# Padding the attention's matmuls of a streaming encoder layer to full 128x128 array tiles

## The chip, the cores and the metric

The kernel runs on one core of a Trainium2 chip. The metric is the device time of one execution in microseconds (us); the time before the change is the median of three runs. TensorE (PE in the profile) multiplies a stationary block, which a weight load (LDWEIGHTS, PEld in the profile) brings into its array of 128 rows and 128 columns, with a moving block that streams past. The contraction runs over the array's rows, the output partitions over its columns. VectorE is DVE, ScalarE is ACT, GpSimd is POOL, and SyncE (SP) issues most transfers.

## The reference

One inference step of one layer (model width 1024). The input is projected once; eight *latent* heads (low-rank keys and values, a rotary key of 32 shared by all heads, mask by chunks of 64) and eight *forgetting* heads (causal, plus a running sum of log forget gates as a bias) attend, both outputs go through one output projection, and a gated feed-forward network follows.

```python
def attend(q, k, v, scale, valid, bias=None):
    s = jnp.einsum('bqhd,bkhd->bhqk', q, k).astype(jnp.float32) * scale
    if bias is not None:
        s = s + bias
    if valid is not None:
        s = jnp.where(valid, s, NEG_INF)
    p = jax.nn.softmax(s, axis=-1).astype(v.dtype)
    return jnp.einsum('bhqk,bkhd->bqhd', p, v)
...
o_a = attend(q_mla, k_mla, v_mla, MLA_SCALE, chunk_mask)
o_b = attend(f_q, f_k, f_v, FOX_SCALE, causal_mask, fox_bias(cum_q, cum_k))
x = x + concat(o_a, o_b) @ w_out
h = rms_norm(x, norm_ffn)
x = x + (silu(h @ w_gate) * (h @ w_up)) @ w_down
```

There are 1072 token columns: 32 new sample rows (with 512 cached keys of their own), 16 meta rows and 1024 prompt rows. The step returns the outputs and the new rows of the caches.

## The kernel before

Every factor is kept as a high and a low part in a reduced 32-bit format, and a product is the sum of three: high by high, high by low, low by high. Heads have a width of 64, so the parts can share the contraction: `fetch` (line 379) loads for each head `a1`, the high query parts twice (128 rows), and `b1`, the high key parts above the low ones (128 rows). One matmul then gives two of the three products. The third, low query by high key, uses `a2`. For a forgetting head `a2` has 70 rows (64 of the low queries and 6 of bias and mask), against `x`. For a latent head `a2` is used with 64 rows, against the upper half of `b1`, and a third matmul of 106 rows adds the rotary part and the masks:

```python
ops = [(a1, b1, 128), (a2, b1, 64), (x, None, 106)]
...
ops = [(a1, b1, 128), (a2, x, 70)]
```

`scores` (line 538) computes the scores of one query tile and one head: the queries are the stationary block, the keys stream past in segments of up to 456 columns. There are nine query tiles (`QT`): the first holds the 48 sample and meta rows, the others 128 prompt rows each. Tile 0 meets 560 keys, tile i meets 16 + 128 i. So a head has 2 segments for tile 0 and 1, 1, 1, 2, 2, 2, 2 and 3 for the others. In forgetting heads line 566 adds a triangle to the last block of 128 (48 in tile 0). DVE then takes the maximum of each row, ACT the exponential with its sum.

`values` (line 593) multiplies the probabilities with the values for a group of query tiles: (5, 6, 7, 8), then (1, 2, 3, 4), then (0,). Each block of 128 keys is transposed on PE (line 624), split in its two parts by ACT and DVE, and multiplied with the values (lines 640 and 641) two blocks later, through a queue. The 16 meta keys come last: a transpose of 32 columns, the low parts laid below the high ones at row 32, and one product of 48 contraction rows (line 638) against the block `v[:, 13]`, which POOL zeroes (line 410) and two transfers fill. Tile 0 has a path of its own: five transposes of 48 rows (line 600) and products of 112 rows (line 610).

`finish_pair` (line 657) divides by the row sums: their inverses are spread and transposed on PE (line 679), 48 rows for tile 0.

`attention` (line 698) runs the heads one after the other: scores of one set of query tiles beside the values of the set before, and beside a *filler*. The forgetting heads go first, with `latent_heads` (line 430: queries, keys and values of the latent heads, line 473 for the values) as their filler; the latent heads follow, with half of the output projection (`out_half`, line 517) as theirs. The operands of a head are fetched one head ahead, in two buffers each, on SP's queue. The forgetting values come from lines 371 to 373, in the input projection before attention.

The order of the work on each engine isn't that of the code: the framework sets it when the program is built, from its own estimate of when each instruction can start.

Of the kernel before, what the change touches and what calls it, by code (L numbers as in the profile page):

```python
# [9 lines left out]
F32 = mybir.dt.float32  # L10
# [13 lines left out]
T = S_NEW + N_META + SEQ          # token columns: [sample new 32 | meta 16 | prompt 1024]  # L24
ODD = S_NEW + N_META              # first query tile: sample and meta rows
NK = PAST + T                     # key columns: [past 512 | token columns]
# [9 lines left out]
NEG = -2.0 ** 100                # exact in every type it passes through  # L36
# [7 lines left out]
OB = 112                          # key block of the first query tile  # L44
# [4 lines left out]
def trunk(ctx: ExitStack, tc: tile.TileContext, a):  # L49
# [30 lines left out]
    zeros = cst.tile([32, 1], F32, name="zeros")  # L80
# [3 lines left out]
    # scratch, each row as its high and its low part: two heads to a row block  # L84
# [12 lines left out]
    # four slots of 128 rows by 4 * T: the normed input, then the mixed heads, then the normed rows of the FFN  # L97
# [8 lines left out]
    def rsqrt(out, ps, n, dim, pool_):  # L106
        """out = (ps / dim + EPS) ** -0.5: exp(-ln / 2), then one Newton step."""
# [38 lines left out]
    # ------------------------------------------------------------ input projection  # L146
# [6 lines left out]
    with ExitStack() as A:  # L153
# [12 lines left out]
        # every weight goes through one ring of [128, 1024] tiles, in the order of its use  # L166
# [5 lines left out]
        def load_w(upto):  # L172
            while len(ring) < min(upto, len(order)):
                name, m, K, n = order[len(ring)]
                if m is None:
                    # the high parts in rows 0:64 of the product, the low ones in rows 64:128
# [27 lines left out]
        # the normed input without its rstd, which comes in after each product  # L204
# [16 lines left out]
        def low_rank(ws, chunks, dim, gain, out, dst, off):  # L221
            """The rows of some chunks: products, RMS norm over the len(ws) row tiles, split into the scratch."""
# [30 lines left out]
        def background(m):  # L253
            """Caches, split on their way to the scratch."""
# [33 lines left out]
        # decoupled key (rows 0:32) and forget gates (rows 32:40)  # L288
# [16 lines left out]
        with tc.tile_pool(name="krl", bufs=1, side="right") as krl:  # L305
# [5 lines left out]
            # log sigmoid: min(z, 0) - log1p(exp(-|z|)), then its running sum  # L311
# [42 lines left out]
        # low-rank queries  # L354
# [4 lines left out]
        # forgetting values, token rows  # L359
        for half in range(2):  # L360
            w = take(2, 1)
            for i, (t0, n) in enumerate(QT):
# [5 lines left out]
                for k in range(8):  # L368
                    s_hi, s_lo = h_hi(k)[:, t0:t0 + n], h_lo(k)[:, t0:t0 + n]
                    hi, lo = (t[:, k % 4] for t in w[k // 4])  # L370
                    pe.matmul(ps[:n, :256], s_hi, hi, start=(k == 0), stop=False)
                    pe.matmul(ps[:n, :256], s_hi, lo, start=False, stop=False)
                    pe.matmul(ps[:n, :256], s_lo, hi, start=False, stop=(k == 7))
# [5 lines left out]
        def fetch(h):  # L379
# [7 lines left out]
            a2 = hp.tile([70, T], FR, tag="a2", name="a2")  # L387
            move(a2[0:64], sQ[p, rw, 1])
            x = hp.tile([128, NK], FR, tag="x", name="x")
            if h < HEADS:  # L390
# [5 lines left out]
                ops = [(a1, b1, 128), (a2, b1, 64), (x, None, 106)]  # L396
# [9 lines left out]
        def fetch_v(h):  # L406
# [3 lines left out]
            pool.tensor_copy(v[:32, 13], zeros.broadcast_to([32, 128]))  # L410
# [6 lines left out]
    # ------------------------------------------------------------ attention  # L417
# [12 lines left out]
    def latent_heads(ev):  # L430
        """Queries, keys and values of the latent heads, in steps of one product, beside the forgetting heads."""
# [14 lines left out]
        def es(n):  # L446
            """One of three buffers, the first in the free end of the slot."""
            turn[0] += 1
            if turn[0] % 3 == 0:
                return lo[:, 3 * T:3 * T + 2 * n].rearrange("p (j t) -> p j t", j=2)  # L450
            return ev.tile([128, 2, 396], FR, tag="es", name="es")
# [5 lines left out]
        for m in range(6):  # L457
# [10 lines left out]
            else:  # L468
                for kt, (k0, n) in enumerate([(128 * i, 128) for i in range(4)] + [(PAST + t0, n) for t0, n in QT]):
                    ps = psF.tile([128, 512], F32, tag="psF", name="psF")  # L470
                    for k in range(2):
                        s_hi, s_lo = l_hi[:, k, k0:k0 + n], l_lo[:, k, k0:k0 + n]
                        pe.matmul(ps[:n, :256], s_hi, w[0][:, k], start=(k == 0), stop=False)
                        pe.matmul(ps[:n, :256], s_hi, w[1][:, k], start=False, stop=False)
                        pe.matmul(ps[:n, :256], s_lo, w[0][:, k], start=False, stop=(k == 1))
# [41 lines left out]
    def out_half(ev):  # L517
        """x plus the output projection of the forgetting heads, beside the latent heads."""
# [19 lines left out]
    def scores(h, ops, i, rs):  # L538
        t0, nq = QT[i]
# [20 lines left out]
        for si, (out, c, w) in enumerate(segs):  # L560
            tri_here = h >= HEADS and si == len(segs) - 1
            for j, (qa, kb, K) in enumerate(ops):
                kb = mixed["B3"] if kb is None else kb
                last = j == len(ops) - 1
                if last and tri_here:
                    pe.matmul(out[:, w - dg:w], identb[:dg, :dg], trib[:dg, :dg], start=False, stop=False)
# [19 lines left out]
    # products with the values run a few blocks behind the transposes that feed them  # L586
# [6 lines left out]
    def values(h, v, tiles, raw):  # L593
        idx = [i for i, _ in tiles]
        po = None
        if idx == [0]:
            P = tiles[0][1]
            pt = psT.tile([128, 512], F32, tag="psT", name="psT")
            for b in range(5):
                pe.transpose(out=pt[:OB, ODD * b:ODD * b + ODD], in_=P[:ODD, OB * b:OB * b + OB], identity=ident[:ODD, :ODD])  # L600
            t0, n = 0, ODD
            # the high and the low parts side by side, through one product
# [11 lines left out]
        else:  # L614
# [3 lines left out]
            blocks.append((0, 32, v[:32 + N_META, 13], 0))  # L618
            for bi, (c, K, vb, imin) in enumerate(blocks):
# [3 lines left out]
                for g in range(g0, len(tiles)):  # L623
                    pe.transpose(out=pt[:K, 128 * g:128 * g + 128], in_=tiles[g][1][:, c:c + K], identity=ident)  # L624
                if meta:
                    # the low parts below the high ones, through one product; the rows between meet rows of zeros
                    hi, lo = tp.tile([128, 512], FR, tag="pth", name="pth"), None
# [415 lines left out]
```

## Time and profile before

| what | us |
|---|---|
| median of three runs | 1614.98 (1611.57 to 1615.22) |
| span of the profiled execution | 1616.5 |
| PE busy in it | 1560.8 (97%) |
| weight loads (PEld) busy | 1439.6 (89%) |
| DVE busy | 981.4 (61%) |
| ACT busy | 594.1 (37%) |
| POOL busy | 215.0 (13%) |

The profile is of one further execution; its own time is known by its span, 1.5 us (0.1%) above the median of the runs. The stages by time: input projection up to 241 us, the forgetting heads up to about 490 us, the latent heads up to about 752 us, then the output projection and the feed-forward network. Each matmul has two records, the weight load and the matmul; records of neighbours overlap, because the next load and the next matmul start before the last one has ended. So a row's length says little, and the distance between the starts of two rows says what one takes of PE. A timeline row merges neighbours of one line (x2); the shape shown is that of the first.

### The profile page before, as it was taken

Reading aid. Unit: us, or ns where it says so; the run is one execution under the profiler, and the core shown is the slowest. Engines: PE = TensorE matmul, PEld = TensorE weight load, DVE = VectorE, ACT = ScalarE, POOL = GpSimd, SP = SyncE. Lnnn points to the kernel's source line nnn. Section 1 sums busy time; section 2 is a strip of 40 time slices with the busy share of each in tenths; the row PEclk is TensorE's granted clock in tenths of the full one; section 3 lists DMA queues with packets and bytes.
Section 4 is the critical chain, followed back from the end, with each engine's and each line's share of the span. In section 5 each row is a group of like instructions: output and inputs, shape, how many; then the busy total and the mean of one; then the engine's idle time right before and its main releaser. Section 6 shows DMA issues by size and latency. Waiting matters only on the chain.

```text
span 1616.5 us, 24215 instructions
## 1 busy us (share of the span) xinstructions
PE 1560.8 (97%) x9273; PEld 1439.6 (89%) x9273; DVE 981.4 (61%) x1843; ACT 594.1 (37%) x1204; POOL 215.0 (13%) x342
## 2 busy tenths in 40 slices
PE   7999998989999999998999999999999999999995
PEld 6999997867886777776999999999999999999995
DVE  7974616757675656566676556565555656565547
ACT  6443436656664555455451111111111111111124
POOL 1344241422231122020000000000000000000014
PEclk9999999989997999999999999999999999999998
DMA  6588667765875654541611111111111111111003
GB/s 186 185 257 291 189 205 223 249 178 165 236 215 139 157 138 116 136 123 41 208 43 40 40 40 40 40 40 65 53 40 40 40 40 40 66 53 39 27 1 109
DMA packets 87827, 183.07 MB, mean 113 GB/s; under 512 B 9690, under 2 KB 53658, under 8 KB 87620
## 3 DMA queue, kind: packets, MB, share of 16 engines
q1 hardware_dynamic: 70784, 127.24, 27.5%
q0 software_dynamic: 16928, 54.29, 9.6%
q8 instruction: 73, 1.20, 0.3%
q14 instruction: 42, 0.34, 0.1%
HBM read 122.83 MB, written 58.67 MB: 112 GB/s over the span
## 4 chain that ended last, share of the span: by engine, by line
PE 82%; DVE 5%; issue 5%; DMA 4%; ACT 2%; POOL 1%; SPq 0%; DVEq 0%; POOLq 0%; ACTq 0%
PE psG L120 11%; PE psG L119 11%; PE psG L121 11%; PE psS L567 7%; PE psD L857 5%; PE psD L856 5%; PE psD L855 5%; PE psT L624 4%; PE psA L121 3%; PE psA L119 3%; PE psA L120 3%; PE po L640 2%; PE po L641 1%; PE psG L810 1%; PE psG L811 1%
## 5 line engine op out<-in xcount | busy, mean ns | idle before, releaser
L864 DVE TENSOR_TENSOR x<-psD,x 128x408 f32<-128x408 f32 (+1 forms) x496 | 236.4, 523 | 5.7 <-PE psD L857 5.7
L119 PE MATMUL psG<-B_hi,gh 128*128 128x408 f32 (+1 forms) x528 | 172.8, 327 | 0.0
L119 PE MATMUL psG<-A_hi,gh 128*128 128x408 f32 (+1 forms) x528 | 172.6, 327 | 0.0
L120 PE MATMUL psG<-A_lo,gh 128*128 128x408 f32 (+1 forms) x528 | 172.6, 327 | 0.0
L120 PE MATMUL psG<-B_lo,gh 128*128 128x408 f32 (+1 forms) x528 | 172.5, 327 | 0.0
L857 PE MATMUL psD<-ah,dl 128*128 128x408 f32 (+1 forms) x528 | 172.1, 326 | 0.0
L121 PE MATMUL psG<-B_hi,gl 128*128 128x408 f32 (+1 forms) x528 | 171.8, 325 | 0.0
L121 PE MATMUL psG<-A_hi,gl 128*128 128x408 f32 (+1 forms) x528 | 171.8, 325 | 0.0
L856 PE MATMUL psD<-al,dh 128*128 128x408 f32 (+1 forms) x528 | 171.7, 325 | 0.0
L855 PE MATMUL psD<-ah,dh 128*128 128x408 f32 (+1 forms) x528 | 170.9, 325 | 0.1
L844 ACT ACTIVATE sl<-sl 128x408 f32<-128x408 f32 (+1 forms) x66 | 33.1, 502 | 353.7 <-DVE sl L843 353.7
L570 DVE TENSOR_REDUCE nm<-psS 128x1 f32<-128x656 f32 (+2 forms) x144 | 104.5, 726 | 73.5 <-PE psS L567 71.7
L567 PE MATMUL psS<-b,a 128*128 128x328 f32 (+4 forms) x360 | 129.9, 383 | 5.1 <-ACT pb L575 4.1
L66 ACT ACTIVATE pth<-psT 128x512 fp32r<-128x512 f32 (+4 forms) x208 | 98.9, 480 | 87.9 <-PE psT L624 75.4
L67 DVE TENSOR_TENSOR ptl<-psT,pth 128x512 fp32r<-128x512 f32 x192 | 104.5, 553 | 40.5 <-ACT pth L66 38.2
L848 DVE TENSOR_TENSOR sq<-psG,rb 128x408 f32<-128x408 f32 (+1 forms) x66 | 34.9, 529 | 151.9 <-PE psG L121 151.9
L795 POOL TENSOR_TENSOR acc<-acc,sq 128x408 f32<-128x408 f32 x14 | 15.0, 1072 | 811.1 <-ACT sq L794 810.4
L843 DVE TENSOR_TENSOR sl<-psG,rb 128x408 f32<-128x408 f32 (+1 forms) x66 | 35.0, 530 | 122.1 <-PE psG L121 122.1
L567 PEld LDWEIGHTS psS<-b,a 128*128 128x128 f32 x360 | 68.6, 191 | 40.3 <-issue 27.0
L66 ACT ACTIVATE ah<-sl 128x408 fp32r<-128x408 f32 (+1 forms) x66 | 33.2, 503 | 187.4 <-DVE sl L849 129.5
L120 PEld LDWEIGHTS psG<-A_lo,gh 128*128 128x128 f32 x528 | 99.3, 188 | 0.5 <-issue 0.3
L855 PEld LDWEIGHTS psD<-ah,dh 128*128 128x128 f32 x528 | 99.2, 188 | 0.5 <-ACT ah L66 0.3
(271 smaller groups left out, 3877.9 us busy)
## 6 DMA issues: line engine op xcount, KB each, us to landing
sg<-w_gu SPq DMA_DIRECT2D x44, 512.0 KB
a<-sQ SPq DMA_DIRECT2D x48, 268.0 KB
b<-sK SPq DMA_DIRECT2D x32, 396.0 KB
sg<-w_down SPq DMA_DIRECT2D x22, 512.0 KB
v<-sV SPq DMA_DIRECT2D x16, 512.0 KB
wst<-w_in SPq DMA_DIRECT2D x13, 512.0 KB
sV<-vt POOLq DMA_DIRECT2D x24, 256.0 KB, 3.8
sV<-A_hi POOLq DMA_DIRECT2D x24, 256.0 KB, 3.4
```

The lines of the kernel that those rows point to most:

```text
L66: act.activation(hi, src, AF.Copy)
L67: eng.tensor_tensor(out=lo, in0=src, in1=f32(hi), op=ALU.subtract)
L119: pe.matmul(ps, whi(k), rhi(k), start=(k == 0), stop=False)
L120: pe.matmul(ps, whi(k), rlo(k), start=False, stop=False)
L121: pe.matmul(ps, wlo(k), rhi(k), start=False, stop=(k == K - 1))
L567: pe.matmul(out, qa[:K, t0:t0 + nq], kb[:K, k0 + c:k0 + c + w], start=(j == 0), stop=last)
L570: dve.tensor_reduce(out=nm[:nq, j:j + 1], in_=src, axis=AX.XY if len(src.shape) == 3 else AX.X, op=ALU.max, negate=True)
L624: pe.transpose(out=pt[:K, 128 * g:128 * g + 128], in_=tiles[g][1][:, c:c + K], identity=ident)
L855: pe.matmul(ps, dh[:, m], ah[:, cs], start=first and j == 0, stop=False)
L856: pe.matmul(ps, dh[:, m], al[:, cs], start=False, stop=False)
L857: pe.matmul(ps, dl[:, m], ah[:, cs], start=False, stop=last and j == len(parts) - 1)
L864: dve.tensor_tensor(out=x2[:, m, cs], in0=ps[:, :n], in1=x2[:, m, cs], op=ALU.add)
```

## The change

Where a matmul of the attention used less than the full array, operands are widened. The contraction of the second score product of latent heads goes from 64 to 128 rows: the low query parts are fetched a second time into rows 64 to 127 of `a2`, so that the product also adds low query by low key, which was left out before. The first query tile is scored for 128 columns; those past 48 aren't used. Tile 0's transposes and those of its row sums read all 128 rows, and overlapping output columns are written over by the next one. The meta keys are transposed in blocks of 128 columns, and their product reads 128 rows: the rows between and below are zeros in `v` and in a block of its own, `meta_hi`, which POOL zeroes once and all meta products share. The stationary blocks of the value projections of 48 columns become 128.

```diff
-    zeros = cst.tile([32, 1], F32, name="zeros")
+    zeros = cst.tile([128, 1], F32, name="zeros")
...
-                    s_hi, s_lo = h_hi(k)[:, t0:t0 + n], h_lo(k)[:, t0:t0 + n]
+                    s_hi, s_lo = h_hi(k)[:, t0:t0 + 128], h_lo(k)[:, t0:t0 + 128]
...
-                    pe.matmul(ps[:n, :256], s_hi, hi, start=(k == 0), stop=False)
+                    pe.matmul(ps[:, :256], s_hi, hi, start=(k == 0), stop=False)
...
-            a2 = hp.tile([70, T], FR, tag="a2", name="a2")
+            a2 = hp.tile([128, T], FR, tag="a2", name="a2")
...
-                ops = [(a1, b1, 128), (a2, b1, 64), (x, None, 106)]
+                move(a2[64:128], sQ[p, rw, 1])
+                ops = [(a1, b1, 128), (a2, b1, 128), (x, None, 106)]
...
-            pool.tensor_copy(v[:32, 13], zeros.broadcast_to([32, 128]))
+            pool.tensor_copy(v[:, 13], zeros.broadcast_to([128, 128]))
...
-                        s_hi, s_lo = l_hi[:, k, k0:k0 + n], l_lo[:, k, k0:k0 + n]
-                        pe.matmul(ps[:n, :256], s_hi, w[0][:, k], start=(k == 0), stop=False)
+                        s_hi, s_lo = l_hi[:, k, k0:k0 + 128], l_lo[:, k, k0:k0 + 128]
+                        pe.matmul(ps[:, :256], s_hi, w[0][:, k], start=(k == 0), stop=False)
...
     def scores(h, ops, i, rs):
-        t0, nq = QT[i]
+        t0, nq = QT[i][0], 128
...
-                    pe.matmul(out[:, w - dg:w], identb[:dg, :dg], trib[:dg, :dg], start=False, stop=False)
+                    pe.matmul(out[:, w - dg:w], identb, trib[:, :dg], start=False, stop=False)
...
+    meta_hi = st.tile([128, 512], FR, name="ptm", bufs=1)
+    pool.tensor_copy(meta_hi, zeros.broadcast_to([128, 512]))
...
-                pe.transpose(out=pt[:OB, ODD * b:ODD * b + ODD], in_=P[:ODD, OB * b:OB * b + OB], identity=ident[:ODD, :ODD])
+                pe.transpose(out=pt[:OB, ODD * b:ODD * b + 128], in_=P[:, OB * b:OB * b + OB], identity=ident)
...
-            blocks.append((0, 32, v[:32 + N_META, 13], 0))
+            blocks.append((0, 32, v[:, 13], 0))
...
-                    pe.transpose(out=pt[:K, 128 * g:128 * g + 128], in_=tiles[g][1][:, c:c + K], identity=ident)
+                    pe.transpose(out=pt[:, 128 * g:128 * g + 128], in_=tiles[g][1][:, c:c + 128], identity=ident)
...
-                    hi, lo = tp.tile([128, 512], FR, tag="pth", name="pth"), None
+                    hi, lo = meta_hi, None
...
-                        pe.matmul(po[:, :W], vb, hi[:32 + N_META, :W], start=False, stop=True)
+                        pe.matmul(po[:, :W], vb, hi[:, :W], start=False, stop=True)
...
-                pe.transpose(out=pt[:, o:o + n], in_=bc[:n, g].rearrange("p a b -> p (a b)"), identity=ident[:n, :n])
+                pe.transpose(out=pt[:, o:o + 128], in_=bc[:, g].rearrange("p a b -> p (a b)"), identity=ident)
```

The program's order moves with it. Rows are the operation, what it writes and reads, and the shape written (x2: two in a row). First, SP's queue, the fetch of one latent head up to its values, before:

```order
L60 DMA a_6329<-sQ 64x1072 x2
L60 DMA b_6332<-sK 64x1584 x2
L60 DMA a_6335<-sQ 64x1072
L60 DMA x<-sQR 32x1072 x3
L60 DMA x<-sM 10x1072
L57 DMA xt<-xT 128x358
L60 DMA v<-sV 112x5x128
```

and with the change:

```order
L60 DMA a_6315<-sQ 64x1072 x2
L60 DMA b_6318<-sK 64x1584 x2
L60 DMA a_6321<-sQ 64x1072
L60 DMA x<-sQR 32x1072 x3
L60 DMA x<-sM 10x1072
L60 DMA a_6321<-sQ 64x1072
L57 DMA xt<-xT 128x356
L57 DMA xt<-xT 128x358
L60 DMA v<-sV 112x5x128
```

The second copy of the low query parts (the last `a`) stands behind the mask rows and ahead of the values `v`; the loads of the filler (`xt` and its weights `wst`) change places around it.

Second, PE in the second forgetting head, where its last meta block is reached, beside the filler (lines 119 to 121). `po` is the output of the values, `psS` the scores, `pth` or `ptm` the transposed probabilities. Before:

```order
L624 MATMUL psT<-ident,pb 128x128 x4
L638 MATMUL po<-pth,v 128x512
L119 MATMUL psF<-A_hi,woh 128x396
L120 MATMUL psF<-A_lo,woh 128x396
L121 MATMUL psF<-A_hi,wol 128x396
L119 MATMUL psF<-A_hi,woh 128x396
L120 MATMUL psF<-A_lo,woh 128x396
L121 MATMUL psF<-A_hi,wol 128x396
L567 MATMUL psS<-b_2576,a_2573 128x272
L566 LDWEIGHTS identb
L566 MATMUL psS<-trib,identb 128x128
```

and with the change (line 638 is line 644 there, 624 is 630, 567 is 568):

```order
L630 MATMUL psT<-ident,pb 128x128 x4
L119 MATMUL psF<-A_hi,woh 128x396
L120 MATMUL psF<-A_lo,woh 128x396
L121 MATMUL psF<-A_hi,wol 128x396
L119 MATMUL psF<-A_hi,woh 128x396
L120 MATMUL psF<-A_lo,woh 128x396
L121 MATMUL psF<-A_hi,wol 128x396
L644 MATMUL po<-ptm,v 128x512
L568 MATMUL psS<-b_2578,a_2575 128x272
L567 LDWEIGHTS identb
L567 MATMUL psS<-trib,identb 128x128
```

The meta product (`po`, 128x512) now stands behind the six products of the filler instead of ahead of them; elsewhere rows change places by a few in the same way, and no stage moves.

## Rows read from the trace of the kernel before

**Rows 1.** The page: its first line and the busy time of each engine.

```profile
span 1616.5 us, 24215 instructions
...
PE 1560.8 (97%) x9273; PEld 1439.6 (89%) x9273; DVE 981.4 (61%) x1843; ACT 594.1 (37%) x1204; POOL 215.0 (13%) x342
```

**Rows 2.** Engines by stretch: length, then busy us of each, clock share, DMA share, GB/s.

```profile
241.00:490.00 249.00, 229.64 (x1395) 190.22 (x1396) 170.37 (x339) 156.28 (x387) 67.30 (x116) 0.95 0.72 211
490.00:752.00 262.00, 259.54 (x1318) 192.30 (x1316) 155.55 (x290) 133.45 (x319) 43.08 (x74) 0.94 0.48 124
...
490.00:530.00 40.00, 38.77 (x153) 27.01 (x152) 22.07 (x42) 17.84 (x42) 7.28 (x10) 0.70 0.55 137
530.00:752.00 222.00, 220.77 (x1167) 165.29 (x1165) 133.49 (x249) 115.61 (x278) 35.80 (x64) 0.98 0.46 122
```

**Rows 3.** Timeline of PE, latent half: start us, us, line, tiles, rows*columns of the stationary block.

```profile
569.98 0.47 PE L600 MATMUL psT<-ident,pa 48*112 48x48 f32 x5
570.38 0.33 PE L640 MATMUL po<-pth,v 128*128 128x128 f32 x1
...
571.58 0.68 PE L567 MATMUL psS<-b,a 128*128 128x346 f32 x2
...
572.45 0.67 PE L567 MATMUL psT<-b,a 128*128 128x348 f32 x2
...
573.32 0.60 PE L679 MATMUL psT<-ident,bc 128*128 128x128 f32 x4
573.85 0.49 PE L638 MATMUL po<-pth,v 48*128 48x512 f32 x1
574.27 0.43 PE L529 MATMUL psF<-B_hi,woh 128*128 128x358 f32 x1
574.54 0.32 PE L530 MATMUL psF<-B_lo,woh 128*128 128x358 f32 x1
...
575.03 0.33 PE L530 MATMUL psF<-B_lo,woh 128*128 128x358 f32 x1
575.19 0.32 PE L531 MATMUL psF<-B_hi,wol 128*128 128x358 f32 x1
```

**Rows 4.** Timeline of PE's weight loads, same half; idle time before them in brackets.

```profile
602.69 0.18 PEld L567 LDWEIGHTS psS<-b,a 64*128 64x128 f32 x1 [0.22 <-issue]
603.04 0.19 PEld L567 LDWEIGHTS psS<-B,x 106*128 106x128 f32 x1 [0.17 <-issue]
```

**Rows 5.** Weight loads by form, whole kernel: busy us, mean ns, then idle us before.

```profile
L567 PEld LDWEIGHTS psS<-x,a 70*128 70x128 f32 x104 | 21.8, 211 | 0.5
L567 PEld LDWEIGHTS psS<-B,x 106*128 106x128 f32 x104 | 20.4, 197 | 17.3 <-issue 14.3
L567 PEld LDWEIGHTS psS<-b,a 64*128 64x128 f32 x104 | 20.0, 193 | 22.4 <-issue 19.4
```

**Rows 6.** Timeline of PE where the first query tile of a latent head is scored.

```profile
588.60 0.39 PE L641 MATMUL po<-ptl,v 128*128 128x512 f32 x1
588.83 0.55 PE L567 MATMUL psS<-b,a 128*48 128x280 f32 x2
...
589.47 0.55 PE L567 MATMUL psS<-b,a 128*48 128x280 f32 x2
...
590.58 0.60 PE L624 MATMUL psT<-ident,pb 128*32 128x128 f32 x4
590.94 0.36 PE L640 MATMUL po<-pth,v 128*128 128x256 f32 x1
```

**Rows 7.** Timeline of PE at the lower clock.

```profile
507.04 0.50 PE L530 MATMUL psF<-B_lo,woh 128*128 128x358 f32 x1
507.34 0.50 PE L531 MATMUL psF<-B_hi,wol 128*128 128x358 f32 x1
```

**Rows 8.** Timeline of SP's queue: the start of two heads' fetches.

```profile
589.80 1.10 SPq L60 DMA_DIRECT2D a<-sQ  x2
...
620.64 1.09 SPq L60 DMA_DIRECT2D a<-sQ  x2
```

More of the change, by code (lines that the diff above doesn't have):

```diff
@@ L368, in trunk @@
                 for k in range(8):
-                    s_hi, s_lo = h_hi(k)[:, t0:t0 + n], h_lo(k)[:, t0:t0 + n]
+                    s_hi, s_lo = h_hi(k)[:, t0:t0 + 128], h_lo(k)[:, t0:t0 + 128]
                     hi, lo = (t[:, k % 4] for t in w[k // 4])
-                    pe.matmul(ps[:n, :256], s_hi, hi, start=(k == 0), stop=False)
-                    pe.matmul(ps[:n, :256], s_hi, lo, start=False, stop=False)
-                    pe.matmul(ps[:n, :256], s_lo, hi, start=False, stop=(k == 7))
+                    pe.matmul(ps[:, :256], s_hi, hi, start=(k == 0), stop=False)
+                    pe.matmul(ps[:, :256], s_hi, lo, start=False, stop=False)
+                    pe.matmul(ps[:, :256], s_lo, hi, start=False, stop=(k == 7))
                 ft = evt.tile([128, 400], F32, tag="et", name="et")
@@ L471, in latent_heads @@
                     for k in range(2):
-                        s_hi, s_lo = l_hi[:, k, k0:k0 + n], l_lo[:, k, k0:k0 + n]
-                        pe.matmul(ps[:n, :256], s_hi, w[0][:, k], start=(k == 0), stop=False)
-                        pe.matmul(ps[:n, :256], s_hi, w[1][:, k], start=False, stop=False)
-                        pe.matmul(ps[:n, :256], s_lo, w[0][:, k], start=False, stop=(k == 1))
+                        s_hi, s_lo = l_hi[:, k, k0:k0 + 128], l_lo[:, k, k0:k0 + 128]
+                        pe.matmul(ps[:, :256], s_hi, w[0][:, k], start=(k == 0), stop=False)
+                        pe.matmul(ps[:, :256], s_hi, w[1][:, k], start=False, stop=False)
+                        pe.matmul(ps[:, :256], s_lo, w[0][:, k], start=False, stop=(k == 1))
                     spill_v(ev, k0, 4 * (m - 4), ps[:n, :256], n, vts[kt % 2])
```

## The prediction

> **What bounds the kernel now.** I read the page first: TensorE (PE) is busy 97% of a span of 1616.5 us [rows 1]. "Busy" is no proof of use, since matmul records overlap; so the second view is the table by stretches. Attention runs from 241 to 752 us, the forgetting heads (8 to 15) up to 490, the latent heads (0 to 7) after that. In the first half PE sits idle for 249.0 - 229.6 = 19.4 us, in the second for only 262.0 - 259.5 = 2.5 us, while DVE is busy for 155.6 and ACT for 133.5 of 262 [rows 2]. So in the latent half nothing but PE is the bound, and what PE does there is worth looking at row by row.
>
> The third view is the timeline of PE, read by starts: the time from one start to the next is what a matmul takes of PE. Two full 128-row products of 358 columns start 575.19 - 575.03 = 0.16 us apart. One score segment of a latent head (three products of 346 columns: 128, 64 and 106 contraction rows; the first two stand in one row, x2) takes 572.45 - 571.58 = 0.87 us, where three at full rate would take 3 x 0.16 = 0.48 [rows 3]. The weight loads say where it goes: the 64-row load starts only after 0.22 us of idle time and the 106-row load behind it after 0.17, both put down to "issue", that is, to nothing the program waits for [rows 4]. Over the kernel the 64-row loads have 22.4 us of idle time before them and the loads behind them 17.3, at 104 each (0.38 us together), while 104 loads of 70 rows, in the same place of the forgetting heads, have 0.5 in all [rows 5]. So between 64 and 70 rows lies a step: a product of at most 64 contraction rows stops the overlap of weight load and matmul on both sides of itself. On the profile, this is a cost of PE alone, and PE is the bound.
>
> **The change part by part.** *Latent scores* (line 567, the second operand from 64 to 128 rows). A latent head has 14 segments in its eight 128-row query tiles (1, 1, 1, 2, 2, 2, 2 and 3), 112 in eight heads. Each gives back 0.87 - 0.48 = 0.39: 43.7 us. The first query tile adds two segments a head, 16 in all; such a segment of 280 columns takes 589.47 - 588.83 = 0.64 [rows 6] against 3 x 0.13 (0.16 scaled by 280/358), so 0.25 each, 4.0 us. The padded rows themselves cost no time: the 70-row products in [rows 5] and the 128-row ones have the same load, and columns set the matmul.
>
> *Meta products* (line 638, 48 rows to 128; two a head, 32). Four transposes take 590.94 - 590.58 = 0.36 before a full product [rows 6] but 573.85 - 573.32 = 0.53 before this one: 0.17. Behind it the next start comes after 0.42, where a 512-column product of 128 rows takes 588.83 - 588.60 = 0.23: 0.19 [rows 3, 6]. The one after that comes 0.27 later instead of 0.16: 0.11. Together 0.47, times 32: 15.0 us.
>
> *First-tile transposes* (line 600, from 48 rows and 48 columns to 128 and 128; 16 groups of five). Now the group takes 570.38 - 569.98 = 0.40 [rows 3], the last hand-over included, with the stall of its first load still ahead of it; five full ones take 5 x 0.09 = 0.45 [rows 6]. The loss of 0.05 and the gain of that stall (at most the 0.17 of a meta product) make -1 to +2 us in all: 0.
>
> *The eight 48-row transposes of line 679 and the eight 48x48 triangle products of line 566*: no clean row; between 0 and the 0.47 of a meta product, I take the 0.25 of a first-tile segment, the nearest small shape: 16 x 0.25 = 4.0 us.
>
> *Narrow stationary blocks* (48 or 32 columns at full contraction: lines 371, 473, the meta transposes of 624, the first-tile scores). A 512-column product hands over to a 48-column block after 0.23, and four 32-column transposes take 0.36, 0.09 each [rows 6]; there is no stall to remove, so 0.
>
> The Trainium skill, "TensorEngine Tiling (Array Packing)", section Key Properties, says that changing the tiling mode drains TensorE, without telling rows from columns. By that the 32 groups of meta transposes would give back another 32 x 0.47 = 15 us or so; the rows of this case show the drain for contraction rows and none for columns, so I don't count it.
>
> Sum on PE: 43.7 + 4.0 + 15.0 + 4.0 = 66.7 us, of which some 56 lie in the latent half (all of the scores, half of the rest) and 10.5 in the forgetting half.
>
> *What is late next.* PE's stalls cover waits for DVE and ACT. Without them the latent half would last 262 - 56 = 206 us with 155.6 us of DVE work in it, 76%; the forgetting half has 170.4 in 249.0, 68%, and there PE idles 19.4 us, 7.8% [rows 2]. At that rate the shorter latent half waits for 16 us, 14 more than now. Of the 10.5 in the forgetting half I let 3 go the same way. The ends: no new waits (gain 66.7), or DVE so late that they are three times as long (66.7 - 51 = 16).
>
> *The added transfer.* Each latent head fetches its low query parts once more, eight moves of 64 rows (268 KB) at the end of the head's fetch on SP's queue, before the values. They wait for the same freed buffer as the move they repeat, so no new wait stands on SP. The fetch of a head starts at 589.8 and the next at 620.6 [rows 8]: 31 us, about 25 afterwards, and the operands are used one head later. At the half's 124 GB/s [rows 2] the move takes 268 KB / 124 = 2.2 us; hidden, 0. Uncovered it would be 8 x 2.2 = 18 us. The zero fills (POOL, 128 rows instead of 32; one more of 512 columns ahead of attention) lie on POOL, busy 43 of 262 us: 0. DVE and ACT on 128 rows instead of 48 see the same columns: 0. The meta block's own single buffer is written again only after four or more other blocks, with its product two blocks behind: no wait.
>
> Net: 66.7 - 14 - 3 = 50 us. The profiled span is 1616.5, the median of the runs 1615.0, 0.1% apart; I take the gain from the median: **1565 us**.
>
> **The rivals.** *(a) Waits come back.* DVE, ACT or the fetches become the bound of the latent half and keep half or more of the gain. For: DVE reaches 76%. Against: the forgetting half works at 68% DVE and loses only 7.8%. Time: gain 16 to 30, so 1585 to 1599.
>
> *(b) The clock comes back too.* In 490 to 530 us PE had 0.70 of its clock, in 530 to 752 us 0.98 [rows 2]. If the denser stream keeps the first stretch at 0.98, some 40 x 0.28 = 11 us more go. Time with few new waits: 1615 - 67 - 5 to 11, so 1537 to 1543.
>
> *(c) Nothing goes.* A 128-row load stalls behind a 128-row product as the 64-row one does, so each segment stays at 0.87. Against: full products start 0.16 apart with all 128 rows in use [rows 3]. Time: 1615, within 5.
>
> The Trainium skill, "TensorE: Matmul & The Clock Gate", Part 3, The mechanism, states such a rule: weight loads overlap with matmuls in flight only when their row groups differ. By that padding, which makes all row groups alike, would win nothing; this case's 0.16 us speaks against it.
>
> *(d) Slower, by the clock.* Once PE outruns DVE in the latent half, it works in bursts with gaps, and the clock falls from 2.4 to 1.2 GHz for long stretches, as it did for part of 490 to 530 us. There two products of 358 columns start 507.34 - 507.04 = 0.30 apart [rows 7] instead of 0.16: each us of full-speed work costs 0.88 us more. It decides from 50 / 0.88 = 57 us of such work on, against some 200 in the half. With half the stage (100 us) at that level: 1615 - 50 + 88 = 1653. Against: the forgetting half has those gaps and a clock of 0.95 [rows 2].
>
> **How the numbers follow.** The forecast has 0.72, (a) 0.12, (b) 0.08, (c) 0.04, (d) 0.04. The likeliest case gives 1565, its own range 1548 (all 66.7) to 1584. The range takes in half of (a) and of (b): 1543 to 1592. About 0.3% (5 us) is what a measurement of this kernel can tell from no change; faster by more: 0.72 + 0.12 + 0.08 = 0.92, within: 0.04, slower: 0.04.
>
> **What would show it.** Right: a 346-column segment takes about 0.48 us from start to start; the idle time before weight loads put down to "issue" falls from 40 us to a few; the latent half shrinks by some 42 us, the forgetting half by 7, the rest stays; DVE's share in the latent half rises to over 70% and PE shows waits for DVE and ACT. Wrong: segments still at 0.87 (c); segments at 0.48 but a latent half over 240 us, with idle time before the scores (a); a granted clock well below 0.94 in the latent half (d).

## The result, and the profile after

The change takes 1568.6 us (median of four runs, 1566.3 to 1572.6), against 1615.1 before (with a fourth run beside the three known earlier): a ratio of 0.9714, with a 95% interval of 0.9688 to 0.9740. That is 46.5 us less; 1565 was forecast. The page of the changed kernel, first line and the engines' busy times:

```profile
span 1567.5 us, 24204 instructions
...
PE 1494.9 (95%) x9273; PEld 1432.9 (91%) x9273; DVE 978.5 (62%) x1843; ACT 594.6 (38%) x1204; POOL 215.8 (14%) x343
```

Beside [rows 1], PE is busy for 66 us less with the same number of matmuls, and the span is 49 us shorter. Engines by stretch (length, busy us of each engine, granted clock, DMA share, GB/s), forgetting half, latent half, and the stretch around the start of the latent half:

```profile
241.00:494.00 253.00, 224.01 (x1424) 194.04 (x1424) 175.24 (x349) 160.02 (x394) 71.73 (x122) 0.97 0.73 216
494.00:704.00 210.00, 200.97 (x1292) 182.95 (x1293) 147.00 (x280) 131.00 (x314) 40.31 (x70) 0.99 0.61 156
490.00:530.00 40.00, 36.01 (x222) 32.43 (x222) 27.84 (x54) 24.41 (x59) 5.34 (x9) 0.96 0.61 161
```

Against [rows 2], PE now stands idle for 253.0 - 224.0 = 29.0 us in the forgetting half (19.4 before) and 9.0 in the latent half (2.5 before). The clock from 490 to 530 us, 0.70 before, is 0.96, that is, nearly all of the stretch at 2.4 GHz. The view of one line gives the halves exactly, by the first and last start of the latent heads' third score product (count, duration min/median/max, starts); before and after:

```profile
L567 PE MATMUL psS<-B,x x120: 287/424/747, 496.3 to 752.2; 106*128 106x328 f32 x16, 106*128 106x392 f32 x16, 106*128 106x456 f32 x16, 106*128 106x346 f32 x16
```

```profile
L568 PE MATMUL psS<-B,x x120: 272/318/448, 494.1 to 703.5; 106*128 106x328 f32 x16, 106*128 106x392 f32 x16, 106*128 106x456 f32 x16, 106*128 106x346 f32 x16
```

The latent half went from 752.2 - 496.3 = 255.9 to 703.5 - 494.1 = 209.4 us, 46.5 less. The forgetting half (from the first score, 241.3 and 241.4) went from 255.0 to 252.7, 2.3 less. Together that is the 49 us between the two profiled spans; the rest of the program took what it took before. Where the 0.87 us of a 346-column segment stood [rows 3], the timeline of PE now has:

```profile
577.23 0.48 PE L568 MATMUL psS<-b,a 128*128 128x346 f32 x2
577.55 0.32 PE L568 MATMUL psS<-B,x 106*128 106x346 f32 x1
577.71 0.48 PE L568 MATMUL psT<-b,a 128*128 128x348 f32 x2
```

577.71 - 577.23 = 0.48 us for three products. And the weight loads of these lines, beside [rows 5] (busy us, mean ns, then idle us before and what ended it):

```profile
L568 PEld LDWEIGHTS psS<-b,a 128*128 128x128 f32 x360 | 65.6, 195 | 15.3 <-ACT pb L576 7.4 <-ACT pa L576 4.8 <-ACT et L375 0.8
...
L568 PEld LDWEIGHTS psS<-x,a 70*128 70x128 f32 x120 | 24.3, 203 | 1.1 <-issue 0.2
L568 PEld LDWEIGHTS psS<-B,x 106*128 106x128 f32 x120 | 22.9, 191 | 0.7
```

The idle time before the second and third product, 22.4 and 17.3 us (19.4 and 14.3 of it put down to "issue"), is gone. The first row holds the first and second products of the latent heads and the first ones of the forgetting heads. Of the 15.3 us left there, 12.2 end with ACT's exponentials `pb` and `pa`: a real wait for a free score bank.

### The profile page after: what moved, and what is told of

Its sections match the earlier page's. It is cut to its first block, busy times and chain, and to the rows that moved or that the text cites. A ratio compares the mean times of both kernels' runs of the same rounds, so it can differ in the third digit from the quotient of the medians.

```text
span 1567.5 us, 24204 instructions
## 1 busy us (share of the span) xinstructions
PE 1494.9 (95%) x9273; PEld 1432.9 (91%) x9273; DVE 978.5 (62%) x1843; ACT 594.6 (38%) x1204; POOL 215.8 (14%) x343
## 4 chain that ended last, share of the span: by engine, by line
PE 80%; DVE 6%; DMA 5%; ACT 4%; issue 3%; POOL 1%; DVEq 0%; SPq 0%; ACTq 0%; POOLq 0%
PE psG L120 11%; PE psG L119 11%; PE psG L121 11%; PE psD L862 5%; PE psD L863 5%; PE psD L861 5%; PE psS L568 4%; PE psT L630 3%; PE psA L121 3%; PE psA L119 3%; PE psA L120 3%; PE po L646 2%; PE po L647 1%; DMA sK<-es 1%; PE psG L816 1%
## 5 line engine op out<-in xcount | busy, mean ns | idle before, releaser
L568 PE MATMUL psS<-b,a 128*128 128x328 f32 (+4 forms) x360 | 103.4, 338 | 9.1 <-ACT pb L576 5.5
L119 PEld LDWEIGHTS psG<-A_hi,gh 128*128 128x128 f32 x528 | 99.2, 188 | 0.5 <-issue 0.2
```

Source lines behind the costliest of these rows:

```text
L119: pe.matmul(ps, whi(k), rhi(k), start=(k == 0), stop=False)
L568: pe.matmul(out, qa[:K, t0:t0 + nq], kb[:K, k0 + c:k0 + c + w], start=(j == 0), stop=last)
```

## The experiments

The theory to be tested: a product of at most 64 contraction rows stops the overlap of load and matmul when PE goes into it and out of it, about 0.39 us a stretch, and PE was the bound where it happened. The rivals: other edits carry the gain; the stall grows with the unused share of the array; any change of tile shape, columns too, costs the same.

**Scores alone.** Only the second score product of the latent heads is padded.

```diff
-            a2 = hp.tile([70, T], FR, tag="a2", name="a2")
+            a2 = hp.tile([128, T], FR, tag="a2", name="a2")
...
-                ops = [(a1, b1, 128), (a2, b1, 64), (x, None, 106)]
+                move(a2[64:128], sQ[p, rw, 1])
+                ops = [(a1, b1, 128), (a2, b1, 128), (x, None, 106)]
```

> Only the second score product of the latent heads is padded from 64 to 128 rows (with its extra transfer); meta products, first-tile transposes and narrow blocks are as before. Theory (a product of at most 64 contraction rows stops the overlap of weight load and matmul on both sides, 0.39 us for each of 112 segments and 0.25 for 16, and about a quarter of it comes back as waits): 47.7 us of PE time go, some 38 of the total: 1577, between 1571 and 1583. Rival (the score products matter little, the gain came from the meta block's own buffer and the other edits): over 1595.

Measured: 1572.0 us, ratio 0.974 (0.9706 to 0.9775). Its interval overlaps that of the whole change. The latent half by the line view, and its engines:

```profile
L568 PE MATMUL psS<-B,x x120: 271/319/392, 496.9 to 705.5; 106*128 106x328 f32 x16, 106*128 106x392 f32 x16, 106*128 106x456 f32 x16, 106*128 106x346 f32 x16
496.90:705.50 208.60, 201.51 (x1282) 177.16 (x1281) 147.39 (x278) 130.12 (x312) 39.98 (x70) 1.00 0.63 159
```

705.5 - 496.9 = 208.6 us, no longer than with every edit. So this one line is nearly all of the change; by the total, the quarter that I let come back as waits was too much; the clock has a part in that (below).

**Everything but the scores.**

```diff
-                move(a2[64:128], sQ[p, rw, 1])
-                ops = [(a1, b1, 128), (a2, b1, 128), (x, None, 106)]
+                ops = [(a1, b1, 128), (a2, b1, 64), (x, None, 106)]
```

> The change with the second score product of the latent heads back at 64 rows. Theory: the 15 us of the 32 meta products and 4 us of small shapes go from PE; the forgetting half returns most of its share as waits (it gained 2.3 us in the change), the latent half keeps its 8: 1605, between 1601 and 1609. Rival (the edits don't add up, the scores only pay with the rest): 1612 to 1617. Second rival (the meta products carry the change): under 1590.

Measured: 1609.6 us, ratio 0.9968 (0.9942 to 0.9995), just outside the expected span. The latent half, by the line view and by its engines:

```profile
L567 PE MATMUL psS<-B,x x120: 284/419/594, 498.3 to 743.5; 106*128 106x328 f32 x16, 106*128 106x392 f32 x16, 106*128 106x456 f32 x16, 106*128 106x346 f32 x16
498.30:743.50 245.20, 243.31 (x1288) 186.34 (x1287) 149.01 (x279) 130.17 (x313) 40.31 (x70) 0.99 0.49 127
```

It lasts 743.5 - 498.3 = 245.2 us, 10.7 less than before, but that profile also has less time at the lower clock (0.99 granted in this half, 0.94 before [rows 2]), and the forgetting half gains nothing. The two parts add up within the noise: 42.5 us and 4.9 us apart, 46.5 together; the 4.9 are largely clock (below). PE at the meta product that stands in [rows 3]:

```profile
568.96 0.60 PE L684 MATMUL psT<-ident,bc 128*128 128x128 f32 x4
569.32 0.48 PE L643 MATMUL po<-ptm,v 128*128 128x512 f32 x1
569.63 0.32 PE L529 MATMUL psF<-B_hi,woh 128*128 128x358 f32 x1
569.79 0.33 PE L530 MATMUL psF<-B_lo,woh 128*128 128x358 f32 x1
```

The three distances are 0.36, 0.31 and 0.16 us, 0.83 together, where they were 0.53 + 0.42 + 0.27 = 1.22: the padding gives back 0.39 us here.

**65 rows instead of 128.**

```diff
-                move(a2[64:128], sQ[p, rw, 1])
-                ops = [(a1, b1, 128), (a2, b1, 128), (x, None, 106)]
+                move(a2[64:65], sQ[p, 64 * (h % 2):64 * (h % 2) + 1, 1])
+                ops = [(a1, b1, 128), (a2, b1, 65), (x, None, 106)]
```

> The change with 65 contraction rows in place of 128 in the second score product: one row of the low query parts is fetched a second time instead of 64 (so one row of low by low products is added instead of 64). Theory (the step lies between 64 and 65 rows, and what lies beyond is free): 1568.6, within 4, with 346-column segments at 0.48 us. Rival (the stall goes with the share of the array that is in use): 0.87 us a segment, near 1605. Second rival (the added transfer of 268 KB a head costs time in the change): 4 to 18 us below 1568.6.

Measured: 1570.0 us, ratio 0.9715 (0.9687 to 0.9743). The timeline of PE, the 65-row loads (busy us, mean ns, idle us before) and the engines in the latent half:

```profile
579.08 0.48 PE L568 MATMUL psS<-b,a 128*128 128x346 f32 x2
579.39 0.33 PE L568 MATMUL psS<-B,x 106*128 106x346 f32 x1
579.56 0.48 PE L568 MATMUL psS<-b,a 128*128 128x346 f32 x2
```

```profile
L568 PEld LDWEIGHTS psS<-b,a 65*128 65x128 f32 x120 | 22.8, 190 | 0.7
```

```profile
497.80:705.80 208.00, 198.98 (x1288) 180.93 (x1288) 146.77 (x279) 130.40 (x313) 40.30 (x70) 1.00 0.56 148
```

0.48 us a segment, and 0.7 us of idle time before 120 loads. It is a step between 64 and 65 rows, and the unused share of the array has no part in it. That the time is the same with one added row as with 64 also shows that the added transfer is hidden.

**Columns alone.** In the kernel before, only the stationary columns become 128 (first-tile scores and value projections from 48, meta transposes from 32). One of the edits:

```diff
-        t0, nq = QT[i]
+        t0, nq = QT[i][0], 128
...
-                    pe.transpose(out=pt[:K, 128 * g:128 * g + 128], in_=tiles[g][1][:, c:c + K], identity=ident)
+                    pe.transpose(out=pt[:, 128 * g:128 * g + 128], in_=tiles[g][1][:, c:c + 128], identity=ident)
```

> The kernel before with only the stationary columns widened: value projections and first-tile scores of 48 columns and meta transposes of 32 columns to 128; all contractions stay as they were (64 and 48 rows). Theory (narrow columns cost nothing at full contraction): 1615, within 4. Rival (every change of the tile shape drains the array, columns too): the 32 groups of meta transposes alone give back some 15 us: 1600 or less.

Measured: 1622.8 us, ratio 1.0043 (1.0020 to 1.0067): a little slower, outside both expectations. The timeline of PE at the first query tile of a latent head:

```profile
586.24 0.61 PE L567 MATMUL psS<-b,a 128*128 128x280 f32 x2
586.78 0.39 PE L567 MATMUL psS<-B,x 106*128 106x280 f32 x1
587.01 0.61 PE L567 MATMUL psS<-b,a 128*128 128x280 f32 x2
```

Such a segment now takes 587.01 - 586.24 = 0.77 us, where it took 0.64 [rows 6]. Wider columns remove no stall; where a 64-row stall stays, they lengthen it by 0.13: each of the two exposed loads brings 128 columns instead of 48 and takes 0.19 to 0.20 us on the mean, where it took 0.12. That is 16 x 0.13 = 2 us. Most of the other 6 goes with the granted clock (0.979 in the middle of these runs, 0.982 before; about 5 us at the rate worked out below); it isn't explained further.

**Fewer stretches, nothing padded.** The kernel before, with the order of the three products changed where a query tile has two or more segments:

```diff
+            seq = ops
+            if h < HEADS and len(segs) > 1 and si < 2:
+                seq = [ops[0], ops[2], ops[1]] if si == 0 else [ops[1], ops[0], ops[2]]
-            for j, (qa, kb, K) in enumerate(ops):
+            for j, (qa, kb, K) in enumerate(seq):
```

> The kernel before, with nothing padded; only the order of the three products of a latent score segment is changed, so that the 64-row products of two segments of one query tile can follow one another: 82 stretches of 64-row products remain of 128. Theory (each entry into and exit from a stretch of 64-row products costs, not the product itself): 46 fewer times 0.37 = 17 us less on PE, most of it on the total: 1599, between 1595 and 1604, with no second stall inside a stretch. Rival (a 64-row product is slow by itself): 1614, within 4.

Measured: 1599.2 us, ratio 0.989 (0.985 to 0.9931). The timeline of PE at one doubled stretch (x3: two products of 64 rows, then one of 128):

```profile
561.71 0.33 PE L570 MATMUL psS<-B,x 106*128 106x346 f32 x1
561.96 0.93 PE L570 MATMUL psS<-b,a 64*128 64x346 f32 x3
562.73 0.33 PE L570 MATMUL psS<-B,x 106*128 106x346 f32 x1
562.90 0.67 PE L570 MATMUL psT<-b,a 128*128 128x348 f32 x2
```

From 561.71 to 562.90 five products of 346 columns take 1.19 us, 0.39 above 5 x 0.16: one stall for two 64-row products. The 15.6 us gained are 46 x 0.34; a product that is slow by itself would have gained none.

**The price by itself.** In the feed-forward network nothing but PE is the bound (from 900 to 1500 us of the changed kernel's profile it is busy for all 600.0). There, for one of eight output tiles, one product of 64 rows, then two, then one of 64 columns:

```diff
+                r = 64 if m == 0 else 128
-                pe.matmul(ps, dl[:, m], ah[:, cs], start=False, stop=last and j == len(parts) - 1)
+                pe.matmul(ps, dl[:r, m], ah[:r, cs], start=False, stop=last and j == len(parts) - 1)
```

```diff
-                pe.matmul(ps, dh[:, m], al[:, cs], start=False, stop=False)
+                pe.matmul(ps, dh[:r, m], al[:r, cs], start=False, stop=False)
```

```diff
-                pe.matmul(ps, dh[:, m], al[:, cs], start=False, stop=False)
+                pe.matmul(ps[:r], dh[:, m, :r], al[:, cs], start=False, stop=False)
```

> The change, and in the feed-forward network, where PE alone is the bound, the third product of the first of eight output tiles uses 64 of its 128 contraction rows (half of the low weight parts times the high activations are left out there): 66 products of 64 rows, each between two products of 128. The price by itself. Theory: 66 x 0.38 = 25 us: 1594, between 1589 and 1599. Rival (the stall belongs to the scores, to their operands or to waits there): 1569, within 4.

> As the run with one 64-row product, but the second and third product of that output tile both use 64 rows (half of both low-order terms is left out there): 132 products of 64 rows in 66 stretches. Theory (cost by entry and exit): as with one, 1594, between 1589 and 1600. Rival (cost by product): twice as much, 1619.

> The change, and in the feed-forward network the second product of the first of eight output tiles uses 64 of its 128 stationary columns at all 128 contraction rows (the low activation parts are left out for 64 of 1024 output rows): 66 narrow products. Theory (narrow columns at full contraction cost nothing): 1568.6, within 4. Rival (every change of the tile shape drains): 1594.

Measured: 1595.0, 1594.0 and 1568.4 us (ratios 0.9859, 0.9858 and 0.9699, intervals within 0.005 of these). The timelines of PE, with one and with two products of 64 rows:

```profile
1004.73 0.28 PE L862 MATMUL psD<-al,dh 128*128 128x256 f32 x1
1004.94 0.38 PE L864 MATMUL psD<-ah,dl 64*128 64x256 f32 x1
1005.25 0.38 PE L861 MATMUL psD<-ah,dh 128*128 128x256 f32 x1
1005.47 0.28 PE L862 MATMUL psD<-al,dh 128*128 128x256 f32 x1
1005.59 0.28 PE L864 MATMUL psD<-ah,dl 128*128 128x256 f32 x1
```

```profile
1008.06 0.28 PE L861 MATMUL psD<-ah,dh 128*128 128x256 f32 x1
1008.27 0.38 PE L863 MATMUL psD<-al,dh 64*128 64x256 f32 x1
1008.50 0.28 PE L864 MATMUL psD<-ah,dl 64*128 64x256 f32 x1
1008.70 0.38 PE L861 MATMUL psD<-ah,dh 128*128 128x256 f32 x1
1008.92 0.28 PE L863 MATMUL psD<-al,dh 128*128 128x256 f32 x1
```

256-column products start 0.12 us apart. With one, 1004.73 to 1005.47 is 0.74 for three, 0.38 above 3 x 0.12: 0.09 on the way in, 0.19 on the way out, 0.10 one product later. With two, 1008.06 to 1008.92 is 0.86 for four, again 0.38. By the runs, 26.4 us / 66 = 0.40 a stretch with one such product, and 25.4 / 66 = 0.38 with two. The narrow product passes without a trace:

```profile
1002.80 0.28 PE L861 MATMUL psD<-ah,dh 128*128 128x256 f32 x1
1002.92 0.28 PE L863 MATMUL psD<-al,dh 128*64 128x256 f32 x1
1003.04 0.28 PE L864 MATMUL psD<-ah,dl 128*128 128x256 f32 x1
```

**Less for PE to do.** The filler products lose one of their three parts (low weights by high activations), in both halves; shown for one of the places:

```diff
                     pe.matmul(ps[:, :n], w[0][:, k], hi[:, k, c0:c0 + n], start=(k == 0), stop=False)
-                    pe.matmul(ps[:, :n], w[0][:, k], lo[:, k, c0:c0 + n], start=False, stop=False)
-                    pe.matmul(ps[:, :n], w[1][:, k], hi[:, k, c0:c0 + n], start=False, stop=(k == 3))
+                    pe.matmul(ps[:, :n], w[0][:, k], lo[:, k, c0:c0 + n], start=False, stop=(k == 3))
```

> The change with one of the three products left out of every filler product in both halves of attention (low weights by high activations, in the keys, values and queries of the latent heads and in the half of the output projection), so that PE has 20.8 us less to do beside the forgetting heads (32 products of 0.18, 52 of 0.118, 54 of 0.164) and 15.7 us less beside the latent heads (96 of 0.164), with the same work for DVE, ACT and the transfers. Theory (after the change both halves wait for DVE and ACT about as much as for PE, which is where the gain of the other edits went): well under half of it shows, the forgetting half by 3 to 10 us, the latent half by 2 to 8: 1552 to 1564. Rival (PE still bounds both halves): 1568.6 - 36 = 1532.

Measured: 1566.9 us, ratio 0.9707 (0.9648 to 0.9766). Of 36.5 us of PE work taken away, 1.7 show (a difference within the spread of the runs), fewer than expected. Engines by stretch (forgetting half, latent half, and the place where the clock is low):

```profile
241.00:494.90 253.90, 210.51 (x1286) 176.58 (x1287) 176.35 (x352) 160.14 (x395) 71.71 (x124) 0.95 0.70 208
494.90:698.80 203.90, 191.41 (x1191) 169.91 (x1192) 145.22 (x276) 129.72 (x311) 39.73 (x68) 0.97 0.66 169
490.00:512.00 22.00, 15.80 (x67) 13.53 (x65) 13.86 (x28) 10.83 (x27) 4.53 (x5) 0.61 0.81 219
```

The forgetting half lasts as long with 20.8 us less to do on PE as with it, and PE stands idle for 253.9 - 210.5 = 43.4 us of it; the latent half is 5.5 shorter with 15.7 less. And the clock fell: 0.980 over the run against 0.989 with the full work, with 0.61 from 490 to 512 us. An engine given less to do waited more and ran slower.

**A second bank for the filler.** In the changed kernel PE's idle time in the forgetting half ends with these, longest in total first (engine and line that waited, releaser, us in total, times, longest):

```profile
PE psF L474 <- DVE A_hi L67: 8.6, 6, 2.1
PE psS L568 <- ACT pb L576: 3.5, 4, 1.5
PE psF L119 <- DVE es L67: 3.0, 4, 1.3
PE psT L606 <- DVE ptm L635: 2.5, 2, 2.2
```

So every second filler product was put in one of the two banks of the transposes:

```diff
+    def filler_bank():
+        fbank[0] += 1
+        if fbank[0] % 2 == 0:
+            return psT.tile([128, 512], F32, tag="psT", name="psT")
+        return psF.tile([128, 512], F32, tag="psF", name="psF")
...
-                    ps = psF.tile([128, 512], F32, tag="psF", name="psF")
+                    ps = filler_bank()
```

> The change, and every second filler product beside the forgetting heads goes to one of the two banks of the transposes (psT) in place of the filler's only bank (psF). Theory one (the forgetting half waits most for the filler's one bank to be emptied by ACT and DVE; PE stands idle some 11 us before those products): the forgetting half falls from 252.6 us by 5 to 12, the total to 1557 to 1564. Theory two (the half is bound by the whole of the chain of ACT and DVE behind all banks, and a bank taken from the transposes is missed there): no gain or a loss, 1566 to 1580.

> As before, with the half of the output projection beside the latent heads sharing the banks of the transposes too. Theory one: the latent half gains a little more, 0 to 4 us beyond the run with the forgetting half alone. Theory two: the latent half loses 2 to 8 us, since its transposes wait for a bank.

Measured: 1605.5 and 1608.8 us (ratios 0.9946 and 0.9971, intervals within 0.003), so 37 and 40 us slower than the change and beyond the spans of both theories. The waits of PE in the forgetting half of the first, its latent heads by the line view, and the engines in its forgetting half:

```profile
PE po L654 <- ACT pth L66: 9.4, 9, 3.3
PE psS L576 <- ACT pb L584: 7.5, 7, 1.9
PE psT L638 <- DVE A_hi L67: 5.6, 4, 3.2
PE psT L638 <- DVE es L137: 5.5, 1, 5.5
```

```profile
L576 PE MATMUL psS<-B,x x120: 272/318/535, 519.5 to 733.6; 106*128 106x328 f32 x16, 106*128 106x392 f32 x16, 106*128 106x456 f32 x16, 106*128 106x346 f32 x16
241.10:519.50 278.40, 233.26 (x1380) 199.34 (x1381) 172.11 (x340) 156.67 (x384) 70.35 (x121) 0.91 0.66 195
```

The wait before `psF` has turned into larger waits for the banks of the transposes (line 638 there) and for the products behind them (`po`); the forgetting half grew to 519.5 - 241.1 = 278 us. The clock fell with it (0.91, where the change has 0.97), so a part of the loss may be the clock's. The latent half took 733.6 - 519.5 = 214 us; in the second run, where the transposes shared their banks there too, it took 215, so 1 us more, where theory two expected 2 to 8. A bank taken from the transposes was missed there, which is the second theory, at a higher price than it named. Whether the filler's one bank limits the half stays open: no run gave the filler a bank that nothing else used.

## Why the prediction was right

**The stall and its place.** The step "between 64 and 70 rows, on both sides, a cost of PE alone" held: 0.87 became 0.48, 65 rows do as well as 128, a stretch costs once, and the price is the same in the feed-forward network (0.38 to 0.40), where scores, waits and operands play no part. Rival (c) is refuted: loads of 128 rows overlap with products of 128 rows in flight, which start 0.12 us apart in the feed-forward network. The rule of the Trainium skill behind it ("TensorE: Matmul & The Clock Gate", Part 3, The mechanism) doesn't hold for these full tiles in the words that the prediction used; the same section excepts loads into a background weight buffer, which no run here can tell apart.

**The scores' term** (43.7 + 4.0) was nearly all of the change: alone, it gave 42.5 us. **The meta products' term** (15.0) was sized too high. I set 0.23 us for a full product of 512 columns, read from one behind another such product; behind transposes it takes 0.31. So a meta product gave back 0.39 instead of 0.47, and 32 of them make 12.5 us by that place. On the total even that hardly shows: with the small shapes the term brought between 3.4 us (whole change against scores alone) and 4.9, neither clear of the clock's differences. The profiles of the scores alone and of the 65 rows, both at a clock of 1.00 in the latent half, have it at 208.6 and 208.0 us. Why so little of it shows there stays open.

**Columns at 0** held: a 64-column product in the feed-forward network costs nothing, and the 15 us that I left out for the meta transposes didn't come with columns alone. The rule of the Trainium skill ("TensorEngine Tiling (Array Packing)", Key Properties) that a changed mode drains TensorE agrees with these runs for rows (0.38 to 0.40 us) and doesn't show in them for columns (1568.4 us with 66 narrow products, 1568.6 without).

**What is late next** was the mis-sized step. I let 3 of 10.5 us come back in the forgetting half; there 8 did (2.3 shown). Even the 2.3 isn't clear: six profiles with the same edits in that half range from 252.0 to 257.1 us. The half was never bound by PE alone: with 20.8 us less work for PE, at a clock of 0.95 for 0.97, it is no shorter. In the latent half I took 14 back from 56 and expected 42; 46.5 showed.

**Rival (b) was no rival but part of the case.** The clock from 490 to 530 us rose from 0.70 to 0.96, a term I had set to 0. The runs of the kernel before give an estimate of its price: in 19 of them on one chip the time goes with the granted clock, from 1609.7 us at 0.987 to 1629.0 at 0.973, so 1.4 us for each 0.001. The middle of these runs has 0.982, that of the changed kernel 0.9895: about 10 of the 46.5 us. A second estimate, from the two profiles: at full clock (length times granted clock) the latent half would last 255.9 x 0.94 = 240.5 us before and 209.4 x 0.99 = 207.3 after, 33 us apart instead of 46.5. Neither is measured apart. By the second one, some 23 of the 56 us of PE time didn't show, where I had let 14 go. Idle time of PE accounts for 6.5 of them (9.0 us against 2.5), less than the 14 I had foreseen as waits; the rest isn't accounted for. The clock that I had left out made up for this, so it is partly luck that the total came within 4 us of the forecast. Whether the denser stream raises the clock by itself stays open: runs of the kernel before, with its 64-row stalls, have it at 0.978 as well as at 0.987. Nor did (a) or (d) come; the shares of DVE and ACT in the latent half are 70% and 62%, about as expected.

Three slips of the sums don't change the forecast. Half of the 19 us beside the scores is 9.5, so the halves hold 57.2 and 9.5 us, not 56 and 10.5. The idle time put down to "issue" was 33.7 us, not 40. The lower end of the range, 1543, is the upper edge of rival (b), so the range took in none of it rather than half.

## What to carry to other kernels

Read PE by starts, not by busy shares, and look for weight loads whose idle time ends with nothing but "issue": a product with at most 64 contraction rows between full ones cost 0.38 to 0.40 us of PE here, as much as two or three full products of 256 to 358 columns, and one more row (or an order that puts such products side by side) gave it back. Pad contractions where PE is the bound, and leave narrow columns alone. Where other engines share the bound, the same kind of saving on PE vanished, and in the run with less work for PE the clock fell.

## What was not expected

The length of the stall depends on the stationary columns (0.25 us with 48, 0.38 with 128, at 280 columns moving), so widening columns beside an unpadded contraction lengthened it; that is some 2 of the 8 us by which that run was slower (1622.8 against 1614.5 us). And 36.5 us less work for PE brought 1.7: the granted clock went from 0.989 to 0.980, which would be 13 us by itself if the 1.4 us for each 0.001, taken from the kernel before, held here too; no run tests that.
